# A decoder trunk: layer 0's feed-forward in three parts, its modulation loads in buffers of their own

## The chip, the cores and the metric

The kernel runs on one core of one Trainium2 chip. The metric is the device time in microseconds (us). Each time is the median of several runs of the same program; lower is better.

## What is computed

Two layers on 256 tokens of width 2048, batch 1. Layer 0 mixes tokens by multi-scale retention, layer 1 by a short gated convolution; each mixer is followed by a SwiGLU feed-forward of inner width 5632. Every sub-layer normalizes x, scales and shifts it by numbers made from a conditioning vector c, and multiplies its output by a gate made from c before it is added to x. These numbers are the modulations: six vectors of 2048 for each layer.

```python
c_act = jax.nn.silu(c)
for i in range(DEPTH):
    mod = (c_act @ w_mod[i] + b_mod[i])[:, None, :]
    sh1, sc1, g1, sh2, sc2, g2 = jnp.split(mod, 6, axis=-1)
    h = (rms_norm(x, norm1_g[i]) * (1.0 + sc1) + sh1).astype(x.dtype)
    ...                                   # i = 0: retention, i = 1: convolution
    x = (x + g1 * y).astype(x.dtype)
    h = (rms_norm(x, norm2_g[i]) * (1.0 + sc2) + sh2).astype(x.dtype)
    a, b = jnp.split(h @ ffn_w_in[i], 2, axis=-1)
    x = (x + g2 * ((jax.nn.silu(a) * b) @ ffn_w_out[i])).astype(x.dtype)
return rms_norm(x, final_g).astype(x.dtype)
```

## The kernel before

All weights lie in one array, `w_all`, in the order of their use, cut into chunks of 128 x 2048 floats (1 MB). SyncE's queue (SP) loads a chunk into a raw buffer. ScalarE (ACT) rounds half of it to a short format, `hi` (L396), and VectorE (DVE) makes the rest, `lo = raw - hi` (L399): one such pair of rows is called a cast here, and a chunk has two. TensorE (PE) multiplies activations, split in the same way, with both. `prepare` keeps two casts ready ahead of PE (`AHEAD`), three in the gathers described below; there are four `hi` and four `lo` buffers.

A modulation is one more 1 MB load, from `w_mod`, and one pass of DVE over it, which multiplies by silu(c) and sums along each row (L312); then one or two tiny POOL instructions. There are 192: 32 in the start stage (L749) and 160 later. Before the change these 160 use the same tag, and so the same three raw buffers (`RAW_BUFS`), as the weight chunks.

When a modulation is issued is set in `paced(n)`, called after each group of products with its column steps n. A column step is one 128 x 128 weight block against all 256 tokens. `plan_mod` gives how many should be done by then, and the allowance grows by `MOST` = 0.045 a column step, is capped at 2, and is set to zero by a group of more than 64 steps. `needed` issues whatever is still missing when a later stage asks for it. The order of PE's instructions is that of the code. Those of the other engines and queues are ordered by a scheduler, in which an L312 has low priority (`MOD_PRIO`).

A feed-forward runs in parts. For a part's tiles (128 inner columns each) the first matrix is multiplied, and then the second with these tiles' rows, whose products are added to x, so x is updated once for each part. The first four tiles (`first_rows`) come with the norm. The others go in gathers of four tiles (`gathered`): eight groups of rows each, two of them (`FIRST_SEVEN`) by seven products in place of eight, for which DVE makes differences of weights (L385, L389, L391). A gather has 20 casts. At a gather's end DVE adds sums (L1165) and multiplies (L1170). PE turns the result (L1179) in the next gather, or after `TURN_ROW` rows of the second matrix. In `gathered` no modulation is issued in groups 1 to 5 (`HELD`). `output` does the second matrix; it starts with four columns at once (`LEAD_FFN`), and updates x by two DVE instructions for each of 16 columns (L665, L666).

Before the change layer 0's two parts have 20 and 24 tiles, so there are four gathers and six. After layer 0's feed-forward come layer 1's norm, its convolution matrices, and its feed-forward in the same two parts. Ahead of that last one the code has these lines, since silu(c) (`cb`) gives its place to other data:

```python
    needed(1, GT2)
    in_cb = const.tile([P, D], F32R, tag="cb", name="in_cb")
```

Of the kernel before, what the change touches and what calls it, by code (L numbers as in the profile page):

```python
# [20 lines left out]
KT = D // P  # L21
DEPTH = 2
# [5 lines left out]
FT = DFF // P  # L28
# [22 lines left out]
RAW_BUFS = 3  # L51
# [49 lines left out]
def out_groups(parts, tail, lead):  # L101

    cols = [c * P for c in range(KT)]
    out = []
    for ks in parts:
        led = cols[:lead]
        out.append([Group(led, ks=ks[:-tail])] + [Group([c], ks=ks[-tail:]) for c in led])
        out[-1] += [Group([c], ks=ks) for c in cols[lead:]]
    return out
# [42 lines left out]
    return [Seven(cols, r) if i in sevens else Group(cols, DV, ks=r) for i, r in rows]  # L152


def ffn_in(sevens):

    n, rows = FFN_TILES[0], [(i, [2 * i, 2 * i + 1]) for i in range(KT // 2)]
    cols = [part * DFF + j * P for j in range(n - 4, n) for part in range(2)]  # L160
    firsts = [Group(cols[:LEAD])] + [Group([c]) for c in cols[LEAD:]]
    fours = [[*range(0, n - 4, 4)], [*range(n, FT, 4)]]
    return firsts, [[in_pairs([j * P, DFF + j * P], rows, sevens) for j in js] for js in fours]


def pair_order(part):

    order = list(range(FFN_TILES[part] // 2))
    if not part:
        a, b = order[-2:]  # L170
        order = order[:5] + [a, order[6], b, order[5], order[7]]
    return [(i, [part * FFN_TILES[0] + 2 * i + n for n in range(2)]) for i in order]


def last_out(part):

    rows = pair_order(part)
# [11 lines left out]
FFN_FIRSTS, FFN_IN = ffn_in(FIRST_SEVEN)  # L189
_, LAST_IN = ffn_in(IN_SEVEN)  # L190
FFN_OUT = out_groups([[k for _, r in pair_order(part) for k in r] for part in range(2)], 2, LEAD_FFN)
LAST_OUT = [last_out(part) for part in range(2)]


def in_use_order():

    for g in RET_SPANS:
        yield "ret_w_in", 0, g
    for n, h in enumerate(HEAD_ORDER):
        qkg, v = RET_HEADS[h]  # L200
        for g in qkg[:2] + [v] + qkg[2:]:
            yield "ret_w_in", 0, g
        if n % (HEADS // 2) == HEADS // 2 - 1:
            for g in RET_OUT[n // (HEADS // 2)]:
                yield "ret_w_out", 0, g
    for layer in range(DEPTH):
        if layer == 1:
            for g in CONV_IN:
                yield "conv_w_in", 0, g
            for g in CONV_OUT:  # L210
                yield "conv_w_out", 0, g
        for part in range(2):
            ins, outs = FFN_IN[part], FFN_OUT[part]
            if layer == DEPTH - 1:
                ins, outs = LAST_IN[part], sum(LAST_OUT[part], [])
            for g in sum(ins, [] if part else FFN_FIRSTS):
                yield "ffn_w_in", layer, g
            for g in outs:
                yield "ffn_w_out", layer, g
# [31 lines left out]
def trunk(ctx: ExitStack, tc: tile.TileContext, x_in, c_in, pos_in, w_mod, cols_in, gain_in, tab_in, w_all, out):  # L251
# [81 lines left out]
    units, allowed, hold = [0], [0.0], [False]  # L333
# [85 lines left out]
    def bank():  # L419
        return ps.tile([P, 2, S], F32, tag="bank", name=name("bank"))  # L420
# [10 lines left out]
    def product(g, act, base=0, before=None, banks=None, last=True):  # L431

        fresh = not banks
        banks = banks or [bank() for _ in g.cols]
        for k in g.ks:
            if before:
                before(k)
            h = act[k - base]
            for c, pt in zip(g.cols, banks):
                hi, lo = take(g, k, c)  # L440
                nc.tensor.matmul(  # L441
                    pt, hi, h, start=fresh and k == g.ks[0], stop=False, skip_group_check=True
                )
                nc.tensor.matmul(  # L444
                    pt[:, 1, :], lo, h[:, 0, :], start=False, stop=last and k == g.ks[-1], skip_group_check=True
                )
# [743 lines left out]
    def first_rows(layer, pairs, turns=()):  # L1190

        pending, done = [], 0
        for i, g in enumerate(FFN_FIRSTS):
# [12 lines left out]
    with tc.tile_pool(name="ffn", bufs=1) as mpool:  # L1206
        first_mid = mids(max(FFN_TILES))[: FFN_TILES[0] // 2]
# [4 lines left out]
        for part in range(2):  # L1212
# [10 lines left out]
            act = [mid[k // 2][:, k % 2] for k in range(2 * n)]  # L1223
            acc = output(
                FFN_OUT[part], act, (0, GT2), part == 1, (lambda j: scaled_only(1, 0, j)) if part else None,
                base=part * FFN_TILES[0], before=lambda k: k == turn_at and waiting.pop(0)(),
            )
    h = rows_at(0)

    mixing = ctx.enter_context(ExitStack())  # L1230
# [31 lines left out]
    mpool.tile([P, 120], F32, tag="apart", name="apart")  # L1262
    h = rows_at(EARLIER)

    first_mid = mids(max(FFN_TILES))[: FFN_TILES[0] // 2]
    xt = [mpool.tile([P, D], F32, tag=f"xt{t}", name=f"xt{t}") for t in range(2)]

    def turn(t, c):
# [130 lines left out]
                nc.vector.tensor_tensor(xs, xs, gain_of[n], op=ALU.mult)  # L1399

    for part in range(2):
        n = FFN_TILES[part] // 2
        mid = mids(FFN_TILES[part]) if part else first_mid
        if not part:
            first_rows(1, mid[-2:], turns)
            tmp("beside_sums", (P, BESIDE_SUMS), bufs=1)
# [8 lines left out]
            ffn_input(groups, mid[2 * i : 2 * i + 2], in_sums, seven)  # L1415
        act = [mid[k // 2][:, k % 2] for k in range(2 * n)]
        for c, groups in enumerate(LAST_OUT[part]):
            last_output(part, 2 * c, groups, act, part * FFN_TILES[0])
    assert not todo


# [34 lines left out]
```

## Time and profile before

| | |
|---|---|
| median of 3 runs | 2633.0 us (2630.23 to 2641.45) |
| the profiled execution | 2635.04 us, span 2633.3 us |
| mean granted TensorE clock | 0.991 |
| busy share of the span | PE 97%, PE's weight loads 84%, DVE 87%, ACT 50%, POOL 5% |
| read from HBM | 685.08 MB, 261 GB/s over the span |

The span is the time from the first to the last instruction; PE is TensorE's matmuls, PEld its weight loads, DVE VectorE, ACT ScalarE, POOL GpSimd. L with a number is a line of the kernel. A granted clock of 1 is TensorE's full speed. A row of the windows view gives a stretch of time, what each engine was busy in it, the granted clock, the share of the DMA engines, and GB/s.

### The profile page before, as it was taken

Reading aid. Unit: us, or ns where it says so; the run is one execution under the profiler, and the core shown is the slowest. Engines: PE = TensorE matmul, PEld = TensorE weight load, DVE = VectorE, ACT = ScalarE, POOL = GpSimd, SP = SyncE. Lnnn points to the kernel's source line nnn. Section 1 sums busy time; section 2 is a strip of 40 time slices with the busy share of each in tenths; the row PEclk is TensorE's granted clock in tenths of the full one; section 3 lists DMA queues with packets and bytes.
Section 4 is the critical chain, followed back from the end, with each engine's and each line's share of the span. In section 5 each row is a group of like instructions: output and inputs, shape, how many; then the busy total and the mean of one; then the engine's idle time right before and its main releaser. Section 6 shows DMA issues by size and latency. Waiting matters only on the chain.

```text
span 2633.3 us, 35134 instructions
## 1 busy us (share of the span) xinstructions
PE 2560.3 (97%) x13563; PEld 2200.0 (84%) x13563; DVE 2297.7 (87%) x2838; ACT 1307.8 (50%) x1726; POOL 135.4 (5%) x232
## 2 busy tenths in 40 slices
PE   7999999999999999999999999999589999999998
PEld 6898889888898788888788998888488888888887
DVE  7988878787799998889998989898889998999978
ACT  5544543444456454344454454444265564565544
POOL 0000000010000000101000000110100000000000
PEclk9999999999999999999999999999789999999999
DMA  9976678777685767867677868887955555455654
GB/s 400 392 285 228 242 262 298 280 275 263 260 296 207 265 256 275 328 242 272 249 268 271 327 236 331 324 327 293 341 217 192 208 204 212 178 214 183 223 208 144
DMA packets 96682, 689.47 MB, mean 262 GB/s; under 512 B 10737, under 2 KB 12161, under 8 KB 13441
## 3 DMA queue, kind: packets, MB, share of 16 engines
q1 hardware_dynamic: 96514, 687.23, 70.1%
q8 instruction: 106, 1.74, 0.3%
q14 instruction: 62, 0.51, 0.0%
HBM read 685.08 MB, written 2.11 MB: 261 GB/s over the span
## 4 chain that ended last, share of the span: by engine, by line
PE 82%; DVE 8%; DMA 5%; issue 2%; ACT 1%; ACTq 0%; DVEq 0%; POOLq 0%; POOL 0%; SPq 0%
PE bank L441 18%; PE bank L455 14%; PE bank L456 14%; PE bank L454 14%; PE bank L444 10%; DMA raw<-w_all 4%; DVE lo L399 3%; PE bank L490 2%; PE bank L489 2%; PE bank L488 2%; DMA raw<-w_mod 1%; PE bank L623 1%; PE bank L621 1%; PE bank L622 1%; ACT hi L396 1%
## 5 line engine op out<-in xcount | busy, mean ns | idle before, releaser
L396 ACT CAST hi<-raw 128x1024 fp32r<-128x1024 f32 (+1 forms) x974 | 983.5, 1024 | 1058.8 <-PE bank L456 373.7
L399 DVE TENSOR_TENSOR lo<-raw,hi 128x1024 fp32r<-128x1024 f32 (+1 forms) x974 | 1142.2, 1186 | 251.6 <-ACT hi L396 245.1
L455 PE MATMUL bank<-lo,h 128*128 128x512 f32 x1592 | 623.9, 392 | 4.6 <-DVE lo L399 4.0
L454 PE MATMUL bank<-hi,h 128*128 128x512 f32 x1592 | 623.6, 392 | 1.1 <-DVE rm L733 1.1
L456 PE MATMUL bank<-hi,h 128*128 128x512 f32 x1592 | 621.2, 390 | 0.0
L312 DVE SCALAR_TENSOR_TENSOR raw<-raw,cb 128x2048 f32<-128x2048 f32 x160 | 364.8, 2285 | 17.6 <-DMA raw<-w_mod 17.2
L455 PEld LDWEIGHTS bank<-lo,h 128*128 128x128 f32 x1592 | 299.4, 188 | 73.0 <-DVE lo L399 14.3
L456 PEld LDWEIGHTS bank<-hi,h 128*128 128x128 f32 x1592 | 299.1, 188 | 62.5
L454 PEld LDWEIGHTS bank<-hi,h 128*128 128x128 f32 x1592 | 299.4, 188 | 61.8 <-DVE rm L733 1.8
L441 PE MATMUL bank<-mid,hi 128*128 128x512 f32 x920 | 319.6, 390 | 0.4 <-ACT hi L396 0.4
L444 PE MATMUL bank<-mid,lo 128*128 128x256 f32 x920 | 259.8, 282 | 1.8 <-DVE lo L399 1.8
L441 PE MATMUL bank<-h,hi 128*128 128x512 f32 x736 | 255.4, 390 | 0.0
L444 PE MATMUL bank<-h,lo 128*128 128x256 f32 x736 | 207.4, 282 | 0.0
L441 PEld LDWEIGHTS bank<-mid,hi 128*128 128x128 f32 x920 | 172.6, 188 | 36.8 <-ACT hi L396 0.8
L444 PEld LDWEIGHTS bank<-mid,lo 128*128 128x128 f32 x920 | 173.9, 189 | 3.2 <-DVE lo L399 3.2
L441 PE MATMUL bank<-rm,hi 128*128 128x512 f32 x496 | 172.5, 390 | 0.0
L441 PEld LDWEIGHTS bank<-h,hi 128*128 128x128 f32 x736 | 138.1, 188 | 29.0
L490 PE MATMUL bank<-h,lo 128*128 128x256 f32 x512 | 146.2, 285 | 4.6 <-DVE lo L399 4.6
L488 PE MATMUL bank<-h,hi 128*128 128x256 f32 x512 | 145.8, 285 | 3.3 <-ACT h L777 3.2
L489 PE MATMUL bank<-h,hi 128*128 128x256 f32 x512 | 145.7, 285 | 0.7 <-DVE h L778 0.7
L444 PE MATMUL bank<-rm,lo 128*128 128x256 f32 x496 | 139.8, 282 | 0.0
L444 PEld LDWEIGHTS bank<-h,lo 128*128 128x128 f32 x736 | 139.1, 189 | 0.0
(273 smaller groups left out, 3427.4 us busy)
## 6 DMA issues: line engine op xcount, KB each, us to landing
raw<-w_all SPq DMA_DIRECT2D x456, 1024.0 KB, 4.9
raw<-w_mod SPq DMA_DIRECT2D x192, 1024.0 KB, 5.0
x<-x_in SPq DMA_DIRECT2D x4, 512.0 KB, 5.2
out<-xt SPq DMA_DIRECT2D x4, 512.0 KB, 3.0
decay<-tab_in SPq DMA_DIRECT2D x8, 128.0 KB, 2.9
x<-gate_row SPq DMA_DIRECT2D x2, 512.0 KB, 4.6
last_gain<-gain_in SPq DMA_DIRECT2D x1, 1024.0 KB, 6.3
cols<-cols_in SPq DMA_DIRECT2D x1, 152.0 KB, 8.3
```

Of the source, the lines that this page charges most:

```text
L312: nc.vector.scalar_tensor_tensor(raw, raw, 1.0, cb, op0=ALU.mult, op1=ALU.mult, accum_out=total)
L396: nc.scalar.copy(hi, raw)
L399: nc.vector.tensor_tensor(lo, raw, hi.bitcast(F32), op=ALU.subtract)
L441: nc.tensor.matmul(pt, hi, h, start=fresh and k == g.ks[0], stop=False, skip_group_check=True)
L444: nc.tensor.matmul(pt[:, 1, :], lo, h[:, 0, :], start=False, stop=last and k == g.ks[-1], skip_group_check=True)
L454: nc.tensor.matmul(o, hi, w_hi, start=first, stop=False)
L455: nc.tensor.matmul(o, hi, w_lo, start=False, stop=False)
L456: nc.tensor.matmul(o, lo, w_hi, start=False, stop=last)
L488: nc.tensor.matmul(pt, hi, h[:, 0, :], start=first, stop=False, skip_group_check=True)
L489: nc.tensor.matmul(pt, hi, h[:, 1, :], start=False, stop=False, skip_group_check=True)
L490: nc.tensor.matmul(pt, lo, h[:, 0, :], start=False, stop=last, skip_group_check=True)
L621: nc.tensor.matmul(pt, hi, high, start=k == 0, stop=False, skip_group_check=True)
```

## The change

Layer 0's feed-forward gets three parts, of 12, 16 and 16 tiles. That makes two gathers, then four, then four: ten as before, but three second matrices in place of two. While it runs, modulations use a raw tag in the stage's own pool, with two buffers, and the weights keep their three; before and after it they share as before. In its second matrices the allowance grows by 0.07 a column step, and `product` calls `paced` every 12 column steps there and no longer once a group. `TURN_ROW` is 5. Layer 1 keeps 20 and 24 tiles. The places of weights in `w_all` follow the new order.

```diff
-FFN_TILES = 20, 24
+FFN_TILES = (12, 16, 16), (20, 24)
+MOD_BUFS = 2
-LEAD_RET, LEAD_CONV, LEAD_FFN, TURN_ROW = 6, 4, 4, 6
+LEAD_RET, LEAD_CONV, LEAD_FFN, TURN_ROW = 6, 4, 4, 5
-MOST = 0.045
+MOST, CATCH_UP = 0.045, 0.07
...
-def pair_order(part):
+def pair_order(tiles, part):
-    order = list(range(FFN_TILES[part] // 2))
+    order = list(range(tiles[part] // 2))
     if not part:
-        a, b = order[-2:]
-        order = order[:5] + [a, order[6], b, order[5], order[7]]
+        *order, a, b = order
+        order = order[:-2] + [a, b] + order[-2:] if len(order) < 8 else order[:5] + [a, order[6], b, order[5], order[7]]
...
-    def mod_raw(t, pool=wpool, bufs=RAW_BUFS):
+    mod_pool = [wpool, RAW_BUFS]
+
+    def mod_raw(t, pool=None, bufs=None):
+        if not pool:
+            pool, bufs = mod_pool
         raw = pool.tile([P, CHUNK], F32, tag="raw", name=name("raw"), bufs=bufs)
         nc.sync.dma_start(raw, w_mod[t])
...
-        allowed[0] = min(allowed[0] + n * MOST, 2.0) if n <= 64 else 0.0
+        allowed[0] = min(allowed[0] + n * most[0], 2.0) if n <= 64 else 0.0
...
     def product(g, act, base=0, before=None, banks=None, last=True):
...
+        counted, at_once = 0, 12 if most[0] > MOST else len(g.cols) * len(g.ks)
         for k in g.ks:
...
             ticked(len(g.cols))
-        paced(len(g.cols) * len(g.ks))
+            counted += len(g.cols)
+            if counted >= at_once:
+                paced(counted)
+                counted = 0
+        if counted:
+            paced(counted)
...
     with tc.tile_pool(name="ffn", bufs=1) as mpool:
+        tiles = FFN_TILES[0]
+        mod_pool[:] = mpool, MOD_BUFS
...
-        for part in range(2):
-            n = FFN_TILES[part] // 2
-            mid = mids(FFN_TILES[part]) if part else first_mid
+        for part, n in enumerate(tiles):
+            mid = mids(n) if part else first_mid
+            last = part == len(tiles) - 1
...
             for i, groups in enumerate(FFN_IN[part]):
                 ffn_input(groups, mid[2 * i : 2 * i + 2], in_sums)
-            ahead_now[0] = AHEAD
+            ahead_now[0], hold[0], most[0] = AHEAD, False, CATCH_UP
...
+            most[0] = MOST
+        mod_pool[:] = wpool, RAW_BUFS
```

Two places where the order of DVE's instructions differs. In these rows L320 is the modulation's pass and L407 the cast's subtraction in the changed kernel (L312 and L399 before); `raw`, `hi` and `lo` are the buffers named above, `x` the trunk's state, `bank` a result of PE.

The first is the end of the convolution's second matrix on DVE, just after its last cast. Before (the first rows of 15 such passes ahead of the next cast):

```order
L399 TENSOR_TENSOR lo_17238<-raw_17207,hi_17237 128x1024
L658 SCALAR_TENSOR_TENSOR x_76<-bank_17206,g_91,x_76 128x256
L312 SCALAR_TENSOR_TENSOR raw_17291,msum_17293<-raw_17291,cb 128x2048
L596 SCALAR_TENSOR_TENSOR h<-x_76,a_84,h 128x256
L312 SCALAR_TENSOR_TENSOR raw_17296,msum_17298<-raw_17296,cb 128x2048
L538 TENSOR_SCALAR rs_17430<-bank_17425 128x2
L312 SCALAR_TENSOR_TENSOR raw_17301,msum_17303<-raw_17301,cb 128x2048
L312 SCALAR_TENSOR_TENSOR raw_17306,msum_17308<-raw_17306,cb 128x2048
```

And now:

```order
L407 TENSOR_TENSOR lo_17364<-raw_17333,hi_17363 128x1024
L680 SCALAR_TENSOR_TENSOR x_76<-bank_17276,g_91,sum_17324 128x256
L320 SCALAR_TENSOR_TENSOR raw_17391,msum_17393<-raw_17391,cb 128x2048
L530 TENSOR_TENSOR acc_16707<-acc_16707,sq_17327 128x256
L610 SCALAR_TENSOR_TENSOR h<-x_76,a_84,h 128x256
L672 SCALAR_TENSOR_TENSOR x_76<-bank_17332,g_91,x_76 128x256
L407 TENSOR_TENSOR lo_17438<-raw_17435,hi_17437 128x1024
```

One pass stands between the last cast of the convolution and the first of layer 1's feed-forward, where 15 stood.

The second is DVE in a gather of the second part, at the second group of differences. Before:

```order
L399 TENSOR_TENSOR lo_10425<-raw_10412,hi_10424 128x1024
L399 TENSOR_TENSOR lo_10438<-raw_10434,hi_10437 128x1024
L399 TENSOR_TENSOR lo_10445<-differences,hi_10444 128x1024
L391 TENSOR_TENSOR raw_10434<-raw_10434 128x512
L399 TENSOR_TENSOR lo_10462<-raw_10434,hi_10461 128x1024
L399 TENSOR_TENSOR lo_10479<-raw_10434,hi_10478 128x512
```

And now:

```order
L407 TENSOR_TENSOR lo_10102<-raw_10089,hi_10101 128x1024
L407 TENSOR_TENSOR lo_10115<-raw_10111,hi_10114 128x1024
L407 TENSOR_TENSOR lo_10122<-differences,hi_10121 128x1024
L397 TENSOR_TENSOR raw_10111<-raw_10111,differences 128x512
L320 SCALAR_TENSOR_TENSOR raw_10570,msum_10572<-raw_10570,cb 128x2048
L407 TENSOR_TENSOR lo_10139<-raw_10111,hi_10138 128x1024
L399 TENSOR_TENSOR raw_10111<-raw_10111 128x512
L320 SCALAR_TENSOR_TENSOR raw_10627,msum_10629<-raw_10627,cb 128x2048
L407 TENSOR_TENSOR lo_10156<-raw_10111,hi_10155 128x512
```

Two passes now stand between the casts of the differences, where there was none; over a gather of the second or third part there are five, and there were three.

More of the change, by code (lines that the diff above doesn't have):

```diff
@@ L152, in in_pairs, with ffn_in @@
     return [Seven(cols, r) if i in sevens else Group(cols, DV, ks=r) for i, r in rows]
[L155 to L159 removed]
+def ffn_in(tiles, sevens):
+    n, rows = tiles[0], [(i, [2 * i, 2 * i + 1]) for i in range(KT // 2)]
     cols = [part * DFF + j * P for j in range(n - 4, n) for part in range(2)]
     firsts = [Group(cols[:LEAD])] + [Group([c]) for c in cols[LEAD:]]
[L162 removed]
+    fours = [[*range(0, n - 4, 4)]]
+    for m in tiles[1:]:
+        fours.append([*range(n, n + m, 4)])
+        n += m
     return firsts, [[in_pairs([j * P, DFF + j * P], rows, sevens) for j in js] for js in fours]
[L166 to L168 removed]
+def pair_order(tiles, part):
+    order = list(range(tiles[part] // 2))
     if not part:
[L170 to L172 removed]
+        *order, a, b = order
+        order = order[:-2] + [a, b] + order[-2:] if len(order) < 8 else order[:5] + [a, order[6], b, order[5], order[7]]
+    return [(i, [sum(tiles[:part]) + 2 * i + n for n in range(2)]) for i in order]
 def last_out(part):
[L177 removed]
+    rows = pair_order(FFN_TILES[-1], part)
     out = []
@@ L186, in last_out @@
     return out
-FFN_FIRSTS, FFN_IN = ffn_in(FIRST_SEVEN)
-_, LAST_IN = ffn_in(IN_SEVEN)
-FFN_OUT = out_groups([[k for _, r in pair_order(part) for k in r] for part in range(2)], 2, LEAD_FFN)
+(FFN_FIRSTS, FFN_IN), (LAST_FIRSTS, LAST_IN) = [ffn_in(*v) for v in zip(FFN_TILES, (FIRST_SEVEN, IN_SEVEN))]
+FFN_ROWS = [[k for _, r in pair_order(FFN_TILES[0], part) for k in r] for part in range(len(FFN_TILES[0]))]
+FFN_OUT = out_groups(FFN_ROWS, 2, LEAD_FFN)
 LAST_OUT = [last_out(part) for part in range(2)]
@@ L211, in in_use_order @@
                 yield "conv_w_out", 0, g
-        for part in range(2):
[L213 to L216, printed above, removed]
+        firsts, parts = FFN_FIRSTS, list(zip(FFN_IN, FFN_OUT))
+        if layer == DEPTH - 1:
+            firsts, parts = LAST_FIRSTS, [(ins, sum(outs, [])) for ins, outs in zip(LAST_IN, LAST_OUT)]
+        for part, (ins, outs) in enumerate(parts):
+            for g in sum(ins, [] if part else firsts):
                 yield "ffn_w_in", layer, g
@@ L1192, in first_rows @@
         pending, done = [], 0
-        for i, g in enumerate(FFN_FIRSTS):
+        for i, g in enumerate(LAST_FIRSTS if layer else FFN_FIRSTS):
             pending += [sums(g)] if i else normed(acc, layer, 1, g)
@@ L1220, in trunk @@
                 ffn_input(groups, mid[2 * i : 2 * i + 2], in_sums)
-            ahead_now[0] = AHEAD
+            ahead_now[0], hold[0], most[0] = AHEAD, False, CATCH_UP
             turn_at = FFN_OUT[part][0].ks[TURN_ROW]
-            act = [mid[k // 2][:, k % 2] for k in range(2 * n)]
+            act = [mid[k // 2][:, k % 2] for k in range(n)]
             acc = output(
-                FFN_OUT[part], act, (0, GT2), part == 1, (lambda j: scaled_only(1, 0, j)) if part else None,
-                base=part * FFN_TILES[0], before=lambda k: k == turn_at and waiting.pop(0)(),
-            )
+                FFN_OUT[part], act, (0, GT2), last, (lambda j: scaled_only(1, 0, j)) if last else None,
+                base=sum(tiles[:part]), before=lambda k: k == turn_at and waiting.pop(0)(),
+            )
+            most[0] = MOST
+        mod_pool[:] = wpool, RAW_BUFS
     h = rows_at(0)
@@ L1401, in trunk @@
     for part in range(2):
-        n = FFN_TILES[part] // 2
-        mid = mids(FFN_TILES[part]) if part else first_mid
+        n = FFN_TILES[-1][part] // 2
+        mid = mids(FFN_TILES[-1][part]) if part else first_mid
         if not part:
```

9 lines of the change are left out of this document (4 added, 5 removed).

## The prediction

> **What bounds the kernel now.** I read the page first, then busy time by stage, then the chain of waits around the one stage that does not fit.
>
> ```profile
> PE 2560.3 (97%) x13563; PEld 2200.0 (84%) x13563; DVE 2297.7 (87%) x2838; ACT 1307.8 (50%) x1726; POOL 135.4 (5%) x232
> PE   7999999999999999999999999999589999999998
> PEclk9999999999999999999999999999789999999999
> PE 82%; DVE 8%; DMA 5%; issue 2%; ACT 1%; ACTq 0%; DVEq 0%; POOLq 0%; POOL 0%; SPq 0%
> ```
>
> TensorE is the bound: 97% busy, 82% of the chain that ended last. The only weak place after the start is slices 28 and 29, where PE falls to five tenths and its granted clock to seven. DVE, at 87%, is the next engine. By stage (us; PE, PEld, DVE, ACT, POOL busy, granted clock, DMA share, GB/s):
>
> ```profile
> 45.00:125.00 80.00, 77.00 (x483) 68.73 (x482) 76.86 (x79) 45.68 (x68) 0.00 (x0) 1.00 1.00 411
> 778.00:825.10 47.10, 47.10 (x367) 45.77 (x367) 42.04 (x71) 32.27 (x63) 2.04 (x3) 1.00 0.62 225
> 1001.60:1114.90 113.30, 112.32 (x649) 99.45 (x650) 93.15 (x103) 44.56 (x46) 8.34 (x20) 1.00 0.80 299
> 1114.90:1378.70 263.80, 261.21 (x1158) 212.83 (x1156) 239.20 (x258) 129.15 (x146) 24.76 (x25) 1.00 0.70 258
> 1378.70:1513.20 134.50, 134.27 (x802) 119.84 (x801) 116.48 (x144) 62.58 (x85) 5.37 (x13) 1.00 0.80 301
> 1549.00:1782.00 233.00, 233.00 (x1346) 206.56 (x1346) 212.65 (x295) 105.71 (x152) 22.46 (x46) 1.00 0.86 319
> 1872.30:1964.70 92.40, 53.51 (x396) 51.44 (x397) 78.64 (x107) 37.57 (x74) 7.28 (x16) 0.78 0.74 282
> ```
>
> Rows two to five belong to layer 0's feed-forward: its first rows, the second matrix of the first part, the six gathers of the second part (263.80/6 = 43.97 us each), and the second matrix of the second part. The sixth row is the convolution's first matrix. The last is layer 1's first rows: the same instructions as in the second row and 32 transposes, yet 92.40 us against 47.10. The chain of waits says what happened there (start, us, what), and the waits and the page's row on L312 say on whom:
>
> ```profile
> 1876.25 2.06 issue
> 1878.79 2.21 DVE raw L312 x2
> 1881.08 2.22 DVE raw L312 x2
> 1883.39 2.31 DVE raw L312 x2
> 1885.72 5.36 DMA raw<-w_mod
> ...
> 1902.37 6.85 DMA raw<-w_mod
> 1909.34 2.31 DVE raw L312 x2
> 1911.67 5.00 DMA raw<-w_all
> 1916.77 1.05 ACT hi L396
> 1917.85 1.24 DVE lo L399
> 1955.90 1.75 PE bank L1272 x16
> 1963.20 1.75 PE bank L1272 x16
> ```
>
> ```profile
> PE bank L621 <- ACT hi L396: 37.8, 2, 37.5
> L312 DVE SCALAR_TENSOR_TENSOR raw<-raw,cb 128x2048 f32<-128x2048 f32 x160 | 364.8, 2285 | 17.6 <-DMA raw<-w_mod 17.2
> ```
>
> The modulations that the pacing had not fitted in by then come here in one run, each a load and an L312 on the same three raw buffers that the weights use. The next weight chunk lands behind them, and PE stands still for 37.5 us. Its clock is then low as well: 0.78 over the stage.
>
> **The change part by part.** All sums are against the profiled execution's own 2635.0 us; it lies 2.0 above the median of 2633.0.
>
> *The run of modulations goes.* In the order of DVE, 15 L312 stand between the convolution's last cast and the next; changed, one does. The stage should then cost what its twin costs, 47.10, and its transposes, twice 1.75: 50.6 instead of 92.40, **-41.8**. That includes the clock's part, since the twin ran at 1.00. Bounds: the 37.5 us wait alone on the small side, 41.8 on the large. I take 41.8, the twin being the same work. The one that is left costs its 2.3 us on DVE and a place among the three raw buffers; I charge **+1**.
>
> *Where they go.* By the order, layer 0's feed-forward now holds 22 more L312 than before (76 for 54), the convolution and its norm 8 fewer. The convolution's are covered on both sides: 233.00 us of PE in 233.00 with 0.86 of the DMA and DVE at 91%. So the price is DVE's, in the feed-forward, and it is highest in the gathers. Before, a gather holds three L312; in the eight gathers of the new second and third parts it holds five. What one costs, and what DVE does else there, is read from the same windows with L312 alone:
>
> ```profile
> 1001.60:1114.90 113.30, 27.48 (x24) 1.00 0.80 299
> 1114.90:1378.70 263.80, 38.51 (x36) 1.00 0.70 258
> ```
>
> An L312 with its accumulator read is 27.48/12 = 2.29 us. A gather without them is (239.20 - 38.51)/6 = 33.45 us of DVE. With five that is 33.45 + 11.45 = 44.9 us in a gather that takes PE 43.97: DVE goes from covered to the bound, by 0.9 us a gather, 7.4 over eight, if it never idles. Packed, the work shrinks a little, as these rows show (start, us):
>
> ```profile
> 1239.38 2.28 DVE L312 SCALAR_TENSOR_TENSOR raw<-raw,cb 128x2048 f32<-128x2048 f32 x1
> 1241.59 2.28 DVE L312 SCALAR_TENSOR_TENSOR raw<-raw,cb 128x2048 f32<-128x2048 f32 x1
> 1243.80 0.68 DVE L1165 TENSOR_TENSOR halves<-bank,halves 128x512 f32<-128x512 f32 x1
> ```
>
> Back to back an L312 takes 2.21, so the overload is 33.45 + 11.05 - 43.97 = 0.5 a gather, 4.2 in all. Against it stands DVE's lead: in a gather three casts are prepared ahead, some 3 x 43.97/20 = 6.6 us, and each of the two runs of four gathers begins with it after a second matrix that has slack. Low end 0. At the high end DVE cannot be filled: the one stretch of the trace where DVE is the bound is 45 to 125 us, at 76.86/80.00 = 0.96. Then a gather is 44.9/0.96 = 46.8, and eight cost 22. I take **+5**, nearer the low end: that start stretch also has the DMA at 1.00, the gathers have it at 0.70.
>
> *Separate buffers for the modulations.* Weights keep three raw buffers, modulations get two of their own until the part ends. The gathers show what sharing costs now:
>
> ```profile
> L385 DVE TENSOR_TENSOR differences<-raw 128x1024 f32<-128x1024 f32 x8 | 9.8, 1224 | 4.2 <-DMA raw<-w_all 4.2
> L455 PE MATMUL bank<-lo,h 128*128 128x512 f32 x224 | 87.9, 392 | 2.0 <-DVE lo L399 1.8
> ```
>
> Over four gathers DVE waits 4.2 us for weights and PE 2.0 for DVE. Removing that is worth 0 to 1 us a gather, 8 at most; a full DVE would eat it, so I count **0**. More bytes move: 8 more loads of 1 MB in 176 us, some 48 GB/s on 258. The convolution's 319 GB/s at no loss covers that. On SP's queue, though, a modulation's load waits until the L312 two before it has run, and the weights behind it wait too; this is a rival below.
>
> *A third part.* It has the same matrix products (eight fewer, wider ones in the last column), but x is read and updated once more: 32 DVE instructions of 0.48 us, 15.4 us.
>
> ```profile
> L665 DVE SCALAR_TENSOR_TENSOR sum<-bank,g,x 128x256 f32<-128x256 f32 x77 | 36.3, 479 | 9.2 <-PE bank L444 8.7
> L666 DVE SCALAR_TENSOR_TENSOR x<-bank,g,sum 128x256 f32<-128x256 f32 x77 | 36.3, 479 | 0.7
> ```
>
> Their cover is the second matrix. The first part's, 12 tiles, takes PE 113.30 x 12/20 = 68 us. DVE has there 24 casts of 1.22 (29.3), the 32 updates (15.4), eight operations of 0.64 left from the gather (two L1170 take 1.28; 5.1), and nine L312 (20.6): 70 us, 2 over, inside the lead. The second part's, 16 tiles, takes PE 90.6, with 39.0 + 15.4 + 5.1 + twelve L312 (27.5) = 87. The third part's holds only four, and is lighter than the fifth row's 116.48 in 134.50. The boundary itself costs: PE is 1.0 us short of the stage in the third row. One more boundary: **+1.5**, between 0 and 3.
>
> *The earlier turn.* TURN_ROW goes from 6 to 5, so PE meets the transposes of the last gather four column steps, 1.4 us, sooner. DVE's product is ready in time:
>
> ```profile
> 1007.00 1.28 DVE L1170 TENSOR_TENSOR halves<-halves,u 128x512 f32<-128x512 f32 x2
> 1011.27 1.04 PE L1179 MATMUL bank<-tab,halves 128*128 128x128 f32 x8
> ```
>
> Ready at 1008.3, used at 1011.3: 3.0 us of slack, 1.6 after. **0**; if DVE is late by the 2 us of one more L312, 0.7 at each of three places.
>
> Sum: 2635.0 - 41.8 + 1 + 5 + 0 + 1.5 + 0 = 2600.7; less the 2.0 by which this execution lies above the median, 2599, which I round to **2600 us**.
>
> [...] In this trace a gap of 37.5 us lowered the clock, while the short waits in the gathers, 2.0 us over four of them, left it at 1.00. [...]
>
> **The rivals.**
>
> *Starved gathers, smaller gain.* If DVE reaches only the 0.96 of the start stretch, the term of 5 becomes 22: 2617. If it reaches no more than the 239.20/263.80 = 0.91 of the gathers now, a gather takes 49.5, and the sum becomes 2600 - 5 + 44 = 2639, no gain at all. For it: DVE's queue runs in order, and in the new order L312 stand between the casts of the differences, where none stood. Against it: DVE's idle time now is mostly the cast waiting because PE has not freed a buffer, which ends when DVE is late.
>
> *Slower: the load queue.* The modulation's load on SP waits for one of two buffers, L312 run late behind full casts, and the weight loads queue behind. If each of the ten gathers had PE wait once for a load as late as that at 1902.37, 6.85 us, the median of 2633 becomes 2633 - 41.8 + 1 + 1.5 + 68.5 = 2662. It decides from 3.9 us a gather, where ten of them eat the gain of 39.3. Against it: a weight chunk feeds two casts, 4.4 us of a gather, and two spare chunks cover 8.8 us, more than that 6.85. The loads stand at most one chunk ahead of their use in the new order.
>
> *The stall stays.* Were the 37.5 us not the run of modulations but the norm's own chain, nothing would be gained: 2633 + 7.5 = 2640. The twin at 47.10 speaks against it, since it has that chain too.
>
> *Better.* Separate buffers give back their 8, the overload is absorbed: 2600 - 5 - 8 = 2587.
>
> **How the numbers follow.** Chances: the sum as made, 2592 to 2610, 0.60; better, 0.10; gathers starved to 0.96 or so, 2610 to 2620, 0.18; starved further, 2620 to 2640, 0.07; slower by the load queue, 0.03; the stall stays, 0.02. The range of 2587 to 2617 reaches from the better case to the starved one's centre and leaves out about 0.2. A measurement of this kernel tells about 0.5%, 13 us. Faster than 2620 are the first three, 0.88; between 2620 and 2646 lie the starved further, the stall that stays and a third of the queue's, 0.10; slower, the rest of the queue's, 0.02.
>
> **What would show it.** Layer 1's first rows should take 50 to 52 us at clock 1.00, with no wait of PE over 3 us. The gathers of the second and third parts should take 44 to 45.5 us with DVE over 95% busy, and five L312 each. The second matrices should keep 0.35 us a column step (113.30/320). Wrong would make it: gathers of 47 us or more, PE waiting on L399 there for over 10 us in all, waits on w_all that grow, or a clock under 1.00 before 1800 us.

## The result, and the profile after

The changed kernel takes 2595.61 us, the median of 4 runs (2593.57 to 2597.39), beside 2635.75 us (4 runs, 2630.23 to 2641.45) for the kernel before on the same chip. The ratio is 0.9849, 95% interval 0.9836 to 0.9862: 1.5% faster. The forecast was 2600, in a range of 2587 to 2617. It was reckoned from a median of 2633.0 before, so it was a gain of 33 us; the gain measured here is 40.

The page of the changed kernel, the lines that answer to those of before (busy time; two lines of tenths by slice; the chain that ended last):

```profile
PE 2559.4 (99%) x13555; PEld 2199.2 (85%) x13555; DVE 2304.6 (89%) x2870; ACT 1312.6 (51%) x1726; POOL 170.3 (7%) x232
PE   7999999999999999999999999999999999999998
PEclk9999999999999999999999999999999999999999
PE 83%; DVE 11%; issue 2%; DMA 2%; ACT 1%; ACTq 0%; POOLq 0%; POOL 0%; DVEq 0%
```

The hole in slices 28 and 29 is gone, in PE and in its clock, and DMA's share of the chain falls from 5% to 2% while DVE's grows from 8% to 11%. PE's busy time is within 1 us of that of before: what went is idle time.

By stage, the rows of the changed kernel (stretch; PE, PEld, DVE, ACT, POOL busy; granted clock, DMA share, GB/s). In order: the two gathers of the first part, its second matrix, the four gathers of the second part, its second matrix, the four gathers of the third, its second matrix, the convolution's first matrix, layer 1's first rows.

```profile
828.20:916.20 88.00, 86.59 (x382) 70.40 (x381) 87.26 (x107) 44.38 (x52) 6.14 (x9) 1.00 0.74 284
916.20:983.70 67.50, 67.50 (x394) 59.88 (x393) 65.73 (x81) 27.43 (x28) 9.57 (x14) 1.00 0.90 341
983.70:1161.90 178.20, 175.02 (x771) 141.44 (x770) 174.14 (x188) 86.06 (x96) 30.91 (x31) 1.00 0.78 301
1161.90:1251.50 89.60, 89.60 (x521) 79.50 (x520) 81.96 (x94) 35.84 (x36) 6.86 (x12) 1.00 0.87 330
1251.50:1429.80 178.30, 175.17 (x770) 141.36 (x769) 175.05 (x188) 86.23 (x97) 30.19 (x29) 1.00 0.81 306
1429.80:1519.60 89.80, 89.80 (x538) 80.29 (x538) 74.88 (x107) 47.34 (x66) 9.20 (x6) 1.00 0.61 219
1555.30:1788.40 233.10, 233.10 (x1347) 206.66 (x1346) 207.55 (x290) 106.83 (x152) 16.24 (x31) 1.00 0.83 304
1877.10:1927.30 50.20, 50.20 (x397) 48.84 (x396) 42.39 (x77) 35.92 (x70) 1.02 (x2) 1.00 0.56 208
```

The time before and after in one table, from such rows of both traces:

| stage | before, us | after, us | difference | predicted |
|---|---|---|---|---|
| up to layer 0's first rows | 778.0 | 781.2 | +3.2 | 0 |
| layer 0's first rows | 47.1 | 47.0 | -0.1 | 0 |
| ten gathers | 440.3 | 444.5 | +4.2 | +5 |
| second matrices | 247.8 | 246.9 | -0.9 | +1.5 |
| convolution: norm and matrices | 359.1 | 357.5 | -1.6 | 0 |
| layer 1's first rows | 92.4 | 50.2 | -42.2 | -40.8 |
| the rest | 668.6 | 668.1 | -0.5 | 0 |

The sum is -37.9 (spans of 2633.3 and 2595.4), against a forecast of -34.3. The first row is code that the change doesn't touch; in the traces of this case it ends anywhere from 778.0 to 781.8 us, so its 3.2 are variation. Without that row the stages gained 41.1. Layer 1's first rows stand at 50.20, PE busy throughout, clock 1.00: twin and transposes, nothing else.

Where the passes went, from the same windows with L320 alone (DVE busy, count with one accumulator read for each pass), and what PE then waits for in the second and third parts' gathers (us in total, times, longest):

```profile
983.70:1161.90 178.20, 43.79 (x40) 1.00 0.78 301
1555.30:1788.40 233.10, 61.93 (x54) 1.00 0.83 304
PE bank L469 <- DVE lo L407: 3.2, 9, 0.8
PE bank L469 <- DVE lo L407: 3.1, 9, 0.9
```

Twenty passes in four gathers, five each. DVE is busy 174.14 of 178.20 us there, 0.977. PE's waits for its casts are all under a microsecond and come to 0.8 us a gather.

### The profile page after: what moved, and what is told of

It reads as the page before. It is cut to its first block, busy times and chain, and to the rows that moved or that the text cites. A ratio compares the mean times of both kernels' runs of the same rounds, so it can differ in the third digit from the quotient of the medians.

```text
span 2595.4 us, 35165 instructions
## 1 busy us (share of the span) xinstructions
PE 2559.4 (99%) x13555; PEld 2199.2 (85%) x13555; DVE 2304.6 (89%) x2870; ACT 1312.6 (51%) x1726; POOL 170.3 (7%) x232
## 4 chain that ended last, share of the span: by engine, by line
PE 83%; DVE 11%; issue 2%; DMA 2%; ACT 1%; ACTq 0%; POOLq 0%; POOL 0%; DVEq 0%
PE bank L450 17%; PE bank L469 15%; PE bank L470 15%; PE bank L468 15%; PE bank L453 9%; DVE lo L407 5%; PE bank L504 2%; PE bank L503 2%; PE bank L502 2%; DVE raw L320 2%; DMA raw<-w_all 1%; PE bank L635 1%; PE bank L637 1%; PE bank L636 1%; DVE raw L763 1%
## 5 line engine op out<-in xcount | busy, mean ns | idle before, releaser
L407 DVE TENSOR_TENSOR lo<-raw,hi 128x1024 fp32r<-128x1024 f32 (+1 forms) x974 | 1142.7, 1186 | 221.0 <-ACT hi L404 215.9
L320 DVE SCALAR_TENSOR_TENSOR raw<-raw,cb 128x2048 f32<-128x2048 f32 x160 | 365.5, 2285 | 12.7 <-DMA raw<-w_mod 12.6
```

The costliest lines, as they stand in the source:

```text
L320: nc.vector.scalar_tensor_tensor(raw, raw, 1.0, cb, op0=ALU.mult, op1=ALU.mult, accum_out=total)
L407: nc.vector.tensor_tensor(lo, raw, hi.bitcast(F32), op=ALU.subtract)
```

## The experiments

In all short diffs, "before" is the kernel before and "after" the changed one; `most[0]` is the growth of the allowance in a column step. A kernel is compared with the kernel before on its own chip, so across chips the ratios are the thing to compare.

**Is the stall the run of modulations?** Before, without its last 15:

```diff
+    todo, n_left = todo[:-15], 15
+    nc.vector.memset(mod_g[1][1], 0.25)
-        while todo and n_mod - len(todo) < due and allowed[0] >= 1.0 and not hold[0]:
+        while todo and n_mod - n_left - len(todo) < due and allowed[0] >= 1.0 and not hold[0]:
```

> The kernel before, in which the last 15 modulations (columns 2 to 16 of layer 1's second gate) are left out, and those gate columns hold a constant; nothing else moves. Theory A (the stall at layer 1's first rows is the run of 15 loads and passes): that stage takes 50 to 51 us at clock 1.00 in place of 92.4, all other stages as before, time 2591 to 2595. Rival (the stall is the norm's own chain or the change of layers): the stage stays above 85 us, time 2630 or more.

Measured: 2592.9 us, ratio 0.9855 (0.9828 to 0.9882). Layer 1's first rows:

```profile
1873.00:1923.30 50.30, 50.30 (x399) 48.93 (x397) 42.60 (x75) 35.96 (x70) 1.64 (x1) 1.00 0.54 206
```

With nothing else changed the stage costs 50.3 us at clock 1.00. The stall was the late modulations and its price was the whole 42 us, the clock's share included. The rival that the norm's own chain makes it is false. The changed kernel does all 160 passes and comes to the same ratio within the intervals, 0.9849.

**Would the pace alone do?** Before, with one constant changed:

```diff
-MOST = 0.045
+MOST = 0.05
```

> The kernel before with one constant changed, MOST 0.045 to 0.05: two parts, shared raw buffers. By the order one pass is left before layer 1's feed-forward (15 before), the gathers hold 3.3 and 3.8 each, the second matrices 13 and 15, the convolution's first matrix 29. Theory A (only the run of late modulations costs, and DVE covers them elsewhere): 33.45 + 3.8 x 2.29 = 42.2 us of DVE in a gather of 44, so no new wait, time 2593 to 2600, equal to the changed kernel within 0.3%. Theory B (in shared buffers each further modulation takes a place from a weight chunk, so PE waits): gathers and second matrices grow, 28 more loads' worth of waits at about 1 us, time 2610 to 2625.

Measured: 2599.64 us, ratio 0.9875 (0.9853 to 0.9897). Its second part's six gathers, the convolution's first matrix, and layer 1's first rows:

```profile
1115.00:1384.10 269.10, 263.99 (x1159) 212.07 (x1157) 249.80 (x268) 130.09 (x147) 21.96 (x24) 1.00 0.75 275
1556.20:1791.70 235.50, 234.15 (x1347) 206.59 (x1346) 219.49 (x300) 106.03 (x151) 19.67 (x42) 1.00 0.87 328
1880.50:1930.70 50.20, 50.20 (x396) 48.83 (x396) 41.33 (x74) 35.86 (x70) 0.71 (x1) 1.00 0.55 203
```

One constant brings the stage to 50.2 us too, with two parts and shared buffers: a ratio of 0.9875 against the change's 0.9849 (the intervals just overlap). It pays more for it: the six gathers go from 263.8 to 269.1 with DVE at only 0.93, and the convolution, with 33 passes in its first matrix for 30, from 233.0 to 235.5. The time is the one that theory A gave, but its "no new wait" is false: the gathers lose 5.3 us with DVE far from full, which is what theory B said of shared buffers, at a smaller price.

**What do the separate buffers do?** After, with its three parts and its pace, but all loads in the three shared buffers:

```diff
-        mod_pool[:] = mpool, MOD_BUFS
...
-        mod_pool[:] = wpool, RAW_BUFS
```

> The changed kernel with the modulations back in the weights' three raw buffers; three parts and CATCH_UP kept. By the order the passes then stand in the second matrices (14, 16, 16) and 3 a gather. Theory A with DVE sums: the first part's second matrix has 29.3 + 15.4 + 5.1 + 14 x 2.29 = 82 us of DVE in 68 of PE, the second's 39 + 15.4 + 5.1 + 36.6 = 96 in 90, so it loses some 10 to 20 us there, gathers 44.0, time 2602 to 2615. Theory B adds weight loads that wait in the second matrices: 2615 to 2630. If the buffers make no difference at all: 2594 to 2598.

Measured: 2627.77 us (10 runs), ratio 0.9977 (0.9965 to 0.9989): nearly all the gain is lost. The last stage is short (50.3 us) and the gathers are within 2 us of the changed kernel's (86.5, 176.5, 179.5 for 88.0, 178.2, 178.3). The three second matrices are not:

```profile
911.90:992.80 80.90, 73.49 (x394) 63.01 (x393) 73.63 (x88) 26.00 (x28) 5.27 (x16) 0.94 0.87 328
1169.30:1269.10 99.80, 92.99 (x522) 80.64 (x521) 90.04 (x102) 35.73 (x38) 3.77 (x15) 0.98 0.91 341
1448.60:1552.00 103.40, 95.85 (x538) 83.45 (x537) 98.47 (x131) 46.93 (x68) 14.87 (x26) 0.95 0.88 324
```

Together they take 284.1 us against 246.9. In the first of them, what the cast on ACT waited for, here and then in the changed kernel:

```profile
ACT hi L404 <- DMA raw<-w_all: 45.6, 11, 8.6
```

```profile
ACT hi L404 <- DMA raw<-w_all: 5.5, 2, 2.8
```

And its chain of waits (start, us, what), where a gap of PE comes from:

```profile
928.31 2.36 DVE lo L407 x2
...
930.69 6.98 DMA raw<-w_all
...
937.77 1.05 ACT hi L404
```

DVE is only 0.91 busy, so it isn't full. With shared buffers a modulation takes a weight chunk's place until its pass has run (in this stage SP's weight loads wait 15.5 us for passes, seven times), and here PE waits for a weight load of 7 us that would otherwise run beside the products. My theory A put this at 2602 to 2615 and missed; theory B held. The buffers, which the sum counted at 0, carry some 34 us at this pace by the ratios; the stages above show 37, because the execution that was profiled is the slowest of the ten (2634.4 us).

The buffers also move passes. With shared buffers 43 passes start in the three second matrices and 31 in the gathers, in the changed kernel 25 and 48. No run keeps the places of the passes and changes the buffers alone, so the 34 us are the price of both together. A kernel below with shared buffers and 31 passes in the second matrices takes 251.4 us for them: sharing costs 4.5 us there at that number.

**And the buffers without the pace?** After, with the second matrices at the old growth:

```diff
-MOST, CATCH_UP = 0.045, 0.07
+MOST, CATCH_UP = 0.045, 0.045
```

> The changed kernel with CATCH_UP at 0.045, so three parts and two buffers of their own, and no higher pace. By the order 9 passes are left before layer 1's feed-forward; gathers hold 4, 5 and 2.75. Theory A: 9 late ones stop PE for 9 x 2.5 = 22 us and the clock falls after it, time 2616 to 2622; the gathers of the second part take 44.5 and those of the third 44.0 us. If few late ones are hidden by the convolution's last casts: under 2605.

Measured: 2615.7 us, ratio 0.9937 (0.9914 to 0.9961). Nine passes are left for the end, and layer 1's first rows and PE's wait there are:

```profile
1872.90:1945.60 72.70, 52.58 (x397) 50.71 (x396) 63.00 (x93) 35.72 (x70) 6.16 (x10) 0.86 0.71 272
PE bank L635 <- ACT hi L404: 19.7, 1, 19.7
```

The time is just under the 2616 to 2622 of theory A. Nine late passes cost 22.5 us of stage where 15 cost 42. In return the third part's gathers, with 10 passes in place of 20, take 173.9 us, not 178.3.

**Neither?** After, with both edits: three parts and `TURN_ROW` of 5 alone.

> Layer 0's feed-forward in three parts and TURN_ROW 5, and nothing else of the change: shared buffers, pace 0.045. By the order 2 to 2.8 passes a gather, 10, 12 and 12 in the second matrices, 9 left at the end. If the third part itself costs little (one more boundary, 1.5 us, and 15.4 us of DVE under the second matrices): gathers 43.9 to 44.1, second matrices 68 + 90 + 90, the late run stops PE for about 22 us as with buffers only, time 2614 to 2620. If the second matrices with shared buffers lose at 0.06 passes a column step (12 in 192) as they did at 0.07: 72 to 80 in the first and 92 to 100 in the others, time 2622 to 2635.

Measured: 2616.39 us, ratio 0.9932 (0.9908 to 0.9955). Again nine passes come late, and the stage takes 74.5 us:

```profile
1874.00:1948.50 74.50, 53.59 (x397) 51.72 (x396) 63.35 (x93) 35.75 (x71) 6.16 (x10) 0.84 0.70 271
```

The four kernels with three parts make a square, by ratio to before:

| | growth 0.045 | growth 0.07 |
|---|---|---|
| shared buffers | 0.9932 | 0.9977 |
| own buffers | 0.9937 | 0.9849 |

Buffers alone bring nothing that these intervals of about 6 us to each side would show, the higher pace alone loses 12 us, both together gain 22 (differences of the ratios, times 2635). The third part itself, with the earlier turn, is worth 16 to 18 us (2632.22 on that chip for before; 0.0068 by the ratio), since 9 passes come late, not 15. Its three second matrices take in 31 passes, the two of before 26. The code gives a reason that no run tests alone: the first group of a second matrix had 72 and 88 column steps before, over the 64 at which the allowance is set to zero, and has 40, 56 and 56 with three parts.

**What stretches the gathers?** After, with a pass over half of each modulation's row while they have their own buffers; the loads stay whole:

```diff
-            nc.vector.scalar_tensor_tensor(raw, raw, 1.0, cb, op0=ALU.mult, op1=ALU.mult, accum_out=total)
+            r, v = (raw, cb) if mod_pool[0] is wpool else (raw[:, :HALF], cb[:, :HALF])
+            nc.vector.scalar_tensor_tensor(r, r, 1.0, v, op0=ALU.mult, op1=ALU.mult, accum_out=total)
```

> The changed kernel in which, during layer 0's feed-forward, a modulation's pass of DVE covers 1024 of its 2048 columns, so half of each sum is left out; loads, buffers and counts stay (9, 22 and 19 passes in the gathers by the order). Theory A (the gathers of the second and third parts are stretched by DVE's work): 33.45 + 5.25 x 1.15 = 39.5 us of DVE a gather, so they fall from 44.6 to 43.5, the value of the third part with 2.5 whole passes a gather (173.9/4). Rival (they are stretched by the loads' place in SP's queue): they stay at 44.4 or more. Time 2588 to 2592 or 2595.

Measured: 2582.17 us (2 runs), ratio 0.9805 (0.9781 to 0.9828). The second part's four gathers, and the pass there:

```profile
979.90:1152.20 172.30, 172.30 (x770) 142.15 (x769) 158.49 (x192) 87.96 (x96) 29.59 (x31) 1.00 0.86 327
L321 DVE SCALAR_TENSOR_TENSOR raw<-raw,cb 128x1024 f32<-128x1024 f32 x23 | 28.0, 1219 | 0.7 <-DMA raw<-w_mod 0.7
```

The DMA is busier than in the changed kernel (0.86 for 0.78), DVE less (0.92 for 0.98), and PE has no gap: 172.30 us busy in 172.30, 43.1 a gather. So DVE's work stretches the gathers, not the loads. (A shorter pass, 1.22 us for 2.28, also frees its buffer sooner; the kernel with one buffer below, where loads wait longer and a gather takes 43.2, speaks against that as the cause.) It costs 5.9 us in four of them, more than the 3.2 of idle PE in the changed kernel's row: the other 2.7 lie inside PE's busy time, 175.02 for the same products. Matmuls overlap in the trace: one of 0.39 us starts every 0.23, so a start that is late by up to 0.16 leaves no gap. In the changed kernel's row 21 starts come over 0.3 us after the one before, 5.9 us beyond the usual 0.23 in all; with half passes three do, by 0.2 us in all. My forecast of 43.5 a gather and 2588 to 2592 had the direction and too small a gain.

**Does the load queue bind?** After, with one buffer for the modulations:

```diff
-MOD_BUFS = 2
+MOD_BUFS = 1
```

> The changed kernel with one buffer for the modulations in place of two. By the order 4 passes a gather (5 with two buffers), 9 in the third part's second matrix (4), 5 in the norm after it. Theory A (DVE's work sets the gathers, and the load queue has slack): 33.45 + 4 x 2.29 = 42.6 us of DVE, gathers 43.6 to 43.9, time 2590 to 2595, not above the changed kernel. Rival, the load queue: with one buffer each load of a modulation waits on SP for the pass just before, weight loads wait behind it, and PE waits on casts as with shared buffers: second matrices of 70 us and more in place of 67.5 and 89.7, time 2600 to 2625.

Measured: 2597.63 us, ratio 0.9865 (0.9844 to 0.9885). The second part's gathers, the convolution's norm, and its first matrix:

```profile
979.50:1152.40 172.90, 172.73 (x771) 141.90 (x770) 167.47 (x180) 87.30 (x96) 37.00 (x31) 1.00 0.77 290
1505.30:1544.30 39.00, 36.31 (x303) 35.90 (x302) 34.96 (x53) 19.91 (x34) 6.66 (x11) 1.00 0.77 277
1544.30:1787.10 242.80, 237.15 (x1346) 208.69 (x1345) 218.57 (x306) 108.59 (x158) 19.29 (x37) 0.99 0.82 308
```

With one buffer only four passes fit in a gather, and it takes 43.2 us with DVE at 0.97. The second matrices are unchanged (67.5, 89.7, 89.7). A stricter wait on SP's queue starves nothing: the load queue is no bound here. Yet the time missed its 2590 to 2595, because passes hang over into the convolution, where they share buffers again: four start in the norm and seven in the first 46 us of the first matrix, two of them in a row. The chain there:

```profile
1553.72 5.14 DMA raw<-w_all
...
1562.30 4.50 DVE raw L320 x4
```

The norm takes 39.0 us for 35.7 and the first matrix 242.8 for 233.1. Nearly all of the matrix's loss lies in its first 46 us, as PE's busy time and clock show:

```profile
1544.30:1590.00 45.70, 40.30 (x212) 34.40 (x211) 43.02 (x68) 19.65 (x38) 8.25 (x12) 0.93 0.75 278
1590.00:1787.10 197.10, 196.84 (x1136) 174.28 (x1135) 175.55 (x239) 88.94 (x120) 11.04 (x25) 1.00 0.84 315
```

It is a loss of the same kind as the old stall, smaller and elsewhere: weight loads and passes in the chain that PE waits for, and a lower clock.

**Can the convolution take more?** After, with a growth of 0.05 in the second matrices and 0.055 in the convolution:

```diff
-MOST, CATCH_UP = 0.045, 0.07
+MOST, CATCH_UP = 0.045, 0.05
...
+    most[0] = 0.055
...
+    most[0] = MOST
```

> The changed kernel with CATCH_UP at 0.05, and MOST at 0.055 from the end of layer 0's feed-forward to layer 1's: by the order 4 passes in a gather of the third part (5), none in its second matrix, 32 in the convolution's first matrix (24), one left at its end. Theory A: the third part's gathers fall to about 43.9 each, 2 to 3 us less in all; the convolution holds 32 with 0 to 2 us lost, since with 33 it took 235.5 in place of 233.0. Time 2592 to 2597: the same as the changed kernel.

Measured: 2602.37 us, ratio 0.9881 (0.9866 to 0.9896), against an expected 2592 to 2597. The third part's gathers become lighter, 176.2 us, but the convolution's first matrix, with 35 passes, pays more:

```profile
1552.70:1793.00 240.30, 235.67 (x1346) 206.52 (x1345) 224.14 (x304) 106.41 (x151) 24.86 (x46) 1.00 0.88 330
```

In the kernel before, this stage takes 30 passes at no loss (233.0). At 33 it took 235.5 in one kernel above, at 35 it takes 240.3. The number is not all: with one buffer it held 30 as well and took 242.8, with seven of them in its first 46 us. (A growth over 0.045 also makes `product` call `paced` every 12 column steps in the convolution, here and in the next experiment; no run separates that.)

**A better version.** One buffer, four passes in a gather, less to catch up in the third part, and what is over spread thinly into the convolution:

```diff
-MOD_BUFS = 2
+MOD_BUFS = 1
-MOST, CATCH_UP = 0.045, 0.07
+MOST, CATCH_UP = 0.045, (0.07, 0.07, 0.03)
...
-            ahead_now[0], hold[0], most[0] = AHEAD, False, CATCH_UP
+            ahead_now[0], hold[0], most[0] = AHEAD, False, CATCH_UP[part]
...
+    most[0] = 0.048
...
+    most[0] = MOST
```

The expectation begins from a neighbour with 0.02 and 0.05, which is described at the end.

> The same with 0.03 in the third part's second matrix and 0.048 in the convolution: 8 passes in that second matrix, 2 in the norm, 28 in the convolution's first matrix. Gathers 43.3 each, the norm 36 to 37.5, the convolution's first matrix 233 to 236: time 2585 to 2591. If two passes hanging over into the norm cost as five did: 2594 to 2598.

Measured: 2590.39 us (2589.17 to 2592.75), ratio 0.9834 (0.9818 to 0.9851). The changed kernel, run beside it on the same chip, gave 2596.21 (2595.71 to 2598.16), so this one is 5.8 us faster and the ranges don't meet. Its second part's gathers and the convolution's second matrix:

```profile
979.30:1152.50 173.20, 173.12 (x771) 141.90 (x770) 167.48 (x180) 87.34 (x96) 37.07 (x31) 1.00 0.79 290
1773.80:1869.30 95.50, 91.42 (x530) 81.00 (x529) 87.31 (x120) 44.47 (x65) 2.32 (x11) 0.96 0.82 302
```

The gathers give back 5 us for four, the norm is at 35.7 and the first matrix at 233.1 with 32 passes. What it loses is in the second row: 11 passes for 9, 95.5 us for 88.7. A neighbour with 0.02 in the third part and 0.05 in the convolution took 2592.98 (2589.66 to 2594.87), just above the expected 2586 to 2591: its first matrix pays 236.3 for 33 passes, its second 94.1. Here is what was expected of it and of the two repeats of the changed kernel, which gave 2595.81 and 2596.21:

> One buffer for the modulations as before, with the pace of the third part's second matrix at 0.02, so that no pass is left for the norm behind it, and 0.05 in the convolution: by the order 4 passes a gather, 8 in the third part's second matrix, none in the norm, 29 in the convolution's first matrix, one at its end. If the loss of the one-buffer kernel behind layer 0 was the passes that hung over into the norm (stalls of PE there, then half clock): the gathers keep 43.3 each (11 us less than the changed kernel), the norm 35.8, the convolution's first matrix 235 to 237, time 2586 to 2591. If it is the number of passes in the convolution with shared buffers: that matrix takes 240 or more, time 2594 to 2600.

> The changed kernel once more, beside the others on this chip, as their measure: 2593 to 2598; gathers 44.0 in the first part and 44.6 in the others.

> The changed kernel beside these two on the same chip: 2593 to 2598.

## Why the prediction was right, point by point

The cause and the largest term were right. That 2595.61 lies so near to 2600 is in part luck: the median of before came out 2.75 us higher in these runs than the one the forecast began from, and in the profiled execution (2597.28 us) the untouched first stage took 3.2 more. By stage, the gain beyond the forecast, 6.8 us without that first stage, is spread over the second matrices (2.4), the convolution (1.6), layer 1's first rows (1.4), the gathers (0.8) and the rest (0.6).

*The run of modulations goes: -41.8 and +1.* The stage fell by 42.2, net of the pass that is left; the two terms came to -40.8. The kernel without the 15 passes shows that this run was the cause. Taking the twin stage as the price, not the 37.5 us wait alone, was right. The +1 for the last pass was not seen: PE is 50.20 us busy in 50.20.

*The gathers: +5.* Measured +4.2. The eight full ones take 44.56 us (178.2 and 178.3 over eight), in the forecast 44 to 45.5, with five passes and DVE at 0.98. The rival of a DVE that can't pass the start stretch's 0.96 is false by that number alone. But the step's baseline was not what I took it for. 43.97 us was not what PE needs; the kernel with half passes shows 43.1. So the gathers before already lost 0.9 us each, and the changed ones lose 1.5 against that floor. The +5 was near because both errors lay in one difference.

*Separate buffers: 0, up to -8.* As a term against the gathers of before this held: ten gathers at the floor would be 431 us, 9 below before, and the full DVE ate it as the step said. As an account of what the buffers do it failed. I looked for their worth in the gathers, where DVE's and PE's waits were listed, and not in the second matrices, where the new pace puts the passes. There they, and the places of the passes that change with them, are worth 37 us (284.1 against 246.9). The sum came out since buffers and pace were changed together; for the pace without the buffers the same working would have been 28 us too low (2600 for 2627.77).

*A third part: +1.5.* The second matrices came to 246.9, 0.9 below before, at 0.35 us a column step (67.50/192, 89.60/256): within a microsecond or two of the bound of 0. The cover was added up to 70 us of DVE in 68 for the first of them. In the changed kernel's groups of instructions in that stage (count, busy, mean ns; idle before) the four largest are:

```profile
L407 DVE TENSOR_TENSOR lo<-raw,hi 128x1024 fp32r<-128x1024 f32 x24 | 29.1, 1217 | 0.9 <-ACT hi L404 0.8
L320 DVE SCALAR_TENSOR_TENSOR raw<-raw,cb 128x2048 f32<-128x2048 f32 x10 | 22.8, 2283 | 0.0
L679 DVE SCALAR_TENSOR_TENSOR sum<-bank,g,x 128x256 f32<-128x256 f32 x15 | 7.0, 479 | 0.7 <-PE bank L453 0.7
L680 DVE SCALAR_TENSOR_TENSOR x<-bank,g,sum 128x256 f32<-128x256 f32 x15 | 7.0, 477 | 0.0
```

With eight operations of 0.68 and the accumulator reads (0.7) they make 72 us, more than the 67.50 that the stage lasts, and the stage's row has DVE busy for 65.73. So the sum of durations was near, and read wrongly: neighbours on a packed DVE overlap, by 6 us over 81 instructions, some 0.08 each. That the third part takes in more passes, worth 16 to 18 us with nothing else changed, stood in no step.

*The earlier turn: 0.* The second matrices show no idle PE in the rows above, so nothing is seen to be lost at the three places. No run changes the turn alone.

*The convolution: 0.* Its first matrix is at 233.10 with 27 passes for 233.00 with 30. By their starts in the traces the whole convolution holds four fewer, not eight, and layer 0's feed-forward 19 more, not 22. That fewer bring nothing in the first matrix is confirmed from the other side: spread out, 32 still took 233.1 and 33 took 235.5. The 1.6 that the convolution gained lie in its second matrix, 88.7 for 90.3.

*The clock.* The prediction read from the trace of before that short waits leave it at 1.00. That is too simple. In the changed kernel's start, a stretch in which PE waits, its two waits from 124 to 130 us, and the stretch behind them:

```profile
124.00:128.00 4.00, 2.47 (x16) 1.79 (x14) 4.00 (x6) 1.05 (x1) 0.00 (x0) 1.00 0.67 277
PE bank L468 <- DVE rm L747: 2.2, 2, 1.4
129.00:132.40 3.40, 3.40 (x16) 3.21 (x15) 3.40 (x4) 2.34 (x5) 0.00 (x0) 0.50 0.91 342
```

Two waits, 2.2 us together and the longer 1.4, and 3.4 us at half speed follow from 129.0 us on. How long a wait has to be for that, no run shows. A sign of being wrong that the prediction named, a clock under 1.00 before 1800 us, did appear, but in code that the change doesn't touch, and not in the two repeats of the changed kernel (mean clock 0.999 there, 0.998 here). The forecast wasn't touched, since the gathers' waits stay at 0.9 us or less and their clock at 1.00.

## What to carry to other kernels

A stage that takes longer than its twin with the same instructions shows at once what a stall costs, the clock's share included, and leaving the suspected work out settles the cause in one run. Work that fills gaps has a price at each place it may go: here 15 passes cost 42 us at the deadline, 4 in the gathers, and nothing in a stage with slack until its buffers run out, so it pays to move each pass to the cheapest place that is left rather than to one pace for all. When a change has several edits, their effects may not add: the pace without buffers lost, the buffers without the pace brought nothing, and one constant in the old kernel gave most of the gain.

## What the runs showed of the hardware that I had not expected

- DVE was kept at 0.977 to 0.982 of a stretch (174.14/178.20, 175.05/178.30) while PE lost 0.8 us in 44.6 to visible waits. Its neighbours overlap by some 0.08 us each, so durations of 72 us fit into 65.73 busy ones.
- A PE that shows as busy may still be late: the same four gathers hold 172.30 us of PE with a light DVE and 175.02 with a full one.
- The clock also fell after waits much shorter than the 37.5 us of before. In the trace of before it is at 0.50 for 41.0 us, from 1882.7 us on, 2.3 us into that wait, until 5.8 us after its end. In the changed kernel's start it is at 0.50 for 3.4 us after waits of 1.4 and 0.8, as above, and with the higher pace in shared buffers from 939.0 to 945.8 us, after one wait of 3.4. The waits in the gathers, of up to 1.1 us before and 0.9 in the changed kernel, left it at 1.00. In the better version, these two waits of PE in the convolution's second matrix, 2.1 and 2.0 us, the second inside the slow stretch, come with 6.8 us at 0.50:

```profile
PE bank L450 <- ACT hi L404: 2.1, 1, 2.1
PE bank L453 <- DVE lo L407: 2.0, 1, 2.0
1809.60:1816.40 6.80, 4.80 (x15) 3.97 (x15) 6.80 (x12) 3.39 (x5) 0.31 (x1) 0.50 0.84 289
```
